# One pipeline over the blocks of the experts, branch hints on four engines, and attention heads in pairs

## The chip, the cores and the metric

The kernel runs on one core of one Trainium2 chip. The metric is the device time in microseconds (us) of one execution. The engines are named as in the profile: PE (TensorE, matmuls and transposes; PEld is its weight load), DVE (VectorE), ACT (ScalarE), POOL (GpSimd), SP (SyncE, which here does little but issue the loads of weights). A name with a q behind it (PEq, DVEq) is that engine's sequencer: branches, register operations and semaphores. All data is float32, for which one matmul shows as two rows of PE; a transpose shows as one.

## The reference, cut to what matters

Two transformer blocks are computed one after the other on 256 tokens of width 1024. The first ends in a mixture of 16 experts, the second has two layers that end in mixtures of 32 experts, over 512 tokens (256 latent, 256 of context) and over 256 tokens. Each token goes to two experts, which the router's scores decide, so how many tokens an expert gets is known only at run time.

```python
def run(args):                       # one block of an expert's tokens
    xb, e = args
    return (jax.nn.silu(xb @ w_gate[e]) * (xb @ w_up[e])) @ w_down[e]
ys = lax.map(run, (xs, block_e)).reshape(cap, d)
return jnp.zeros((n + 1, d), x.dtype).at[slot_tok].add(ys * slot_w[:, None])[:n]
```

w_gate and w_up are 1024x512, w_down is 512x1024: 6 MiB of weights for an expert. The second layer's mixer is an attention with 16 heads of 64: eight query heads that share two heads of keys and values (GQA), and eight "neighbourhood" heads with keys of their own and a bias for each offset in a window. Every head has 256 queries and 512 keys (256 of context, 256 latent):

```python
s = jnp.einsum('bkgqd,bksd->bkgqs', q, k, preferred_element_type=jnp.float32) * ATTN_SCALE
p = jax.nn.softmax(s, axis=-1).astype(v.dtype)
return jnp.einsum('bkgqs,bksd->bkgqd', p, v)
```

## The kernel before, in words

**Stages.** The profiled execution goes through: the first block's mixer and memory attention (0 to about 430 us), its 16 experts (MoE1, to about 745), the conv mixers of the second block (to about 945), 32 experts on 512 tokens (MoE2, to about 1537), projections, the attention (about 1686 to 1774) and its output, then 32 experts on 256 tokens (MoE3, to 2248) and the last combination. In this trace 22 of MoE3's 32 experts have tokens.

**Weights.** SP loads weights in pieces of 1 MiB into a ring of buffers (ring, ringb, and in the MoEs also nrm, x1c and hcT), in a planned order (plan_moe, L1092): for each expert two halves of gate, two of up, two of down. A piece is loaded as soon as its buffer has been given back (ring.free) by an expert that is done with it. For MoE3 (skip=True) the used experts come first in the order, and a load is left out where the count is zero.

**An expert** works on its tokens in blocks of 32. block_up (L1142) multiplies a block's columns with gate and up, 32 matmuls into four column groups of one PSUM bank, and copies the result to a tile u on DVE. block_mid (L1154) turns u on PE (L1158), applies Silu on ACT (L1160), and multiplies on DVE (L1161) into hd. block_down (L1165) is 16 matmuls (L1169) and a copy to a tile y (L1173 on ACT or L1175 on DVE); block 0 is written by a plain DMA that ACT issues (L1177), later blocks by an indirect DMA on POOL (L1179), to places that depend on the counts. There are 105 blocks in this execution: 8 of MoE1's 16 experts have two, 13 of MoE2's 32 have two or three. Token rows come by indirect DMAs (gather, L1205) for four experts at a time and are turned on PE by columns (L1220); a block beyond the second (and the second of MoE3's expert 3) picks its rows by a matmul with a selection matrix instead (columns_32, L1329).

**Branches.** more (L1344) holds the blocks beyond the first in nested Ifs, up to four deep; every engine with instructions in it takes the branch (L1346). The down of block b is passed into the If of block b+1 and stands there behind that block's up; where there is no further block it stands in the Else, or, for the first block of an expert, behind a second branch (L1413, n < 33). ahead (L1340) gives PE alone a hint which way a coming branch will go. In MoE1, MoE2 and for the first three experts of MoE3 the up of the next expert's first block comes ahead of that branch at L1413, so a single-block expert's down runs behind the next expert's up. In the rest of MoE3 every expert stands in an If of its own (L1392, in groups of four under L1432), with its up, its mid and its down in a row, and unused positions are branched over one by one, with their columns (L1220) still done.

**Attention.** 20 steps; step i does the scores of head i (two 64-row matmuls of 512 keys, L2126, and for neighbourhood heads two matmuls that add the bias, L2128), the softmax pieces on DVE and ACT (L2130, L2131), the eight transposes of head i-1 (L2141, copied by ACT L2144 and DVE L2146), the eight value matmuls of head i-2 (L2156, scaled by DVE L2158) and, for every second head, two transposes into oT (L2165).

Of the kernel before, what the change touches and what calls it, by code (L numbers as in the profile page):

```python
# [11 lines left out]
I32 = mybir.dt.int32  # L12
# [78 lines left out]
LAG = (1, 2, 3)  # L91
# [43 lines left out]
def body(tc, a, dbg=lambda n, ap: None, stop=99):  # L135
# [3 lines left out]
    with es:  # L139
# [952 lines left out]
        def plan_moe(m, E, wa, wb, wc, key, after=None, skip=False):  # L1092
# [30 lines left out]
        def moe(m, wa, wb, wc, key, hook=lambda: None, after=lambda e: None, gmul=None, skip=False):  # L1123
# [6 lines left out]
            EQ = E // 4  # L1130
            yb, ya = yslots[0:2 * NT, :], yslots[D:D + 32 * E, :]
# [10 lines left out]
            def block_up(XT, w, tag="u"):  # L1142
# [7 lines left out]
                u = q.tile([128, 256], F32, tag=tag, name="u", bufs=1)  # L1150
# [3 lines left out]
            def block_mid(u, b):  # L1154
# [4 lines left out]
                hd = q.tile([128, 2, 64], F32, tag=f"hd{b}", name="hd", bufs=1)  # L1159
                S.activation(hd, pv[:, :, 0:64], AF.Silu)  # L1160
                V.tensor_tensor(hd, hd, pv[:, :, 64:128], ALU.mult)  # L1161
                return hd[:, 0], hd[:, 1]

            def block_down(hd, w, e, b):
                p = ps("c")  # L1165
                for k in (0, 2, 1, 3):
                    for g in range(4):
                        c = (k % 2) * 1024 + 256 * g
                        T.matmul(p[32 * g:32 * g + 32, 0:256], hd[k % 2][:, 32 * (k // 2):32 * (k // 2) + 32], w[k // 2][:, c:c + 256],  # L1169
# [6 lines left out]
                if b == 0:  # L1176
                    S.dma_start(ya[32 * e:32 * e + 32, :].rearrange("s (g c) -> g s c", g=4), y)  # L1177
                else:
                    G.indirect_dma_start(out=yb.rearrange("r (g c) -> (r g) c", g=4), out_offset=bass.IndirectOffsetOnAxis(ap=iy[:, b - 1, e:e + 1], axis=0),  # L1179
                                         in_=y, in_offset=None, bounds_check=8 * NT - 1, oob_is_err=False)  # L1180
# [33 lines left out]
            def columns(n, XT, sl=slice(0, 128)):  # L1214
                rowsg.remove(n)
                r = gathered[n % 2]
                pa = [ps("c"), ps("c")]
# [27 lines left out]
            u0 = block_up(XTs[0][:, :, 0:32], up_w)  # L1245
# [6 lines left out]
            iy = q.tile([128, NB, E], I32, name="iy")  # L1252

            def blocks():
# [35 lines left out]
                for b in range(NB):  # L1290
                    V.tensor_scalar(iy[:, b, :], obp, 128.0, scol[:, b:b + 1], op0=ALU.mult, op1=ALU.add)
                V.reduce_max(cnt[:, E:], cnt[:, :E], axis=AX.X)
# [7 lines left out]
            def places():  # L1300
                tm = q.tile([128, 256], F32, tag="u", name="tm", bufs=1)[:, :nt * 2 * E].rearrange("p (t k e) -> p t k e", t=nt, k=2)
# [38 lines left out]
            def ahead(e, b, n):  # L1340

                tc.mark_branch_hint_location(f"{key}_{e}_{b}", hint=n > 32 * b, engines=[ET.PE])

            def more(e, b, n, w, w2_, before, other=True):  # L1344

                with tc.If(n > 32 * b, label=f"{key}_{e}_{b}") as cmp:  # L1346
                    if b < NB:
                        ahead(e, b + 1, n)
                    if b == 1 and not (skip and e == 3):
                        u = block_up(XT1[:, :, 32 * (e % 4):32 * (e % 4) + 32], w, "ux")  # L1350
                        before()
                    else:
                        u = block_up(columns_32(e, b, before), w, "ux")
# [15 lines left out]
            def expert(e, up_w, u0, n=None):  # L1369

                i, j = e // 4, e % 4
                by_use = skip and e >= 3
                old = len(due) if by_use else 9
                n1 = None
                if not by_use:
                    dn_w = get(2)
                    hd = block_mid(u0, 0)
                if e == 0:
                    n, n1 = used(0), used(1)
                    ahead(0, 1, n)  # L1380
                    up_1 = get(4)
                    u0 = block_up(XTs[0][:, :, 32:64], up_1)
# [3 lines left out]
                sure = n is not None  # L1386
                n = n if sure else used(e)
                if not by_use:
                    more(e, 1, n, up_w, dn_w, lambda: block_down(hd, dn_w, e, 0), False)
                else:  # L1390
                    up_w, dn_w = get(4), get(2)
                    with ExitStack() if sure else tc.If(n > 0):  # L1392
                        ahead(e, 1, n)
                        hds = block_mid(block_up(XTs[i % 2][:, :, 32 * j:32 * j + 32], up_w), 0)
                        more(e, 1, n, up_w, dn_w, lambda: block_down(hds, dn_w, e, 0))
# [4 lines left out]
                if e == 0:  # L1400
                    up_w = up_1
                    ahead(1, 1, n1)
                elif e + 1 < (3 if skip else E):
                    up_w = get(4)
                    n1 = used(e + 1)
                    ahead(e + 1, 1, n1)
                    u0 = block_up(XTs[((e + 1) // 4) % 2][:, :, 32 * ((e + 1) % 4):32 * ((e + 1) % 4) + 32], up_w)
# [4 lines left out]
                if not by_use:  # L1412
# [862 lines left out]
```

## Time and profile before

| what | value |
| --- | --- |
| median of 3 runs | 2274.81 us (2269.14 to 2281.2) |
| profiled execution | 2280.37 us, span 2278.6 us |
| mean granted clock of PE | 0.88 of full speed |
| busy, share of the span | PE 78%, weight load 49%, DVE 27%, ACT 12%, POOL 11% |
| moved by DMA | 636.5 MB, mean 279 GB/s |

Shares over the whole span say little here, because the stages have different limits: the MoEs stream weights, the stages between them compute on what is there. So the views are read stage by stage.

### The profile page before, as it was taken

The page shows a single profiled execution, that of the slowest core. Times are in us where ns is not written, and L with a number is a line of the kernel's source. Part 1 is how long each engine was busy: PE and PEld are TensorE (multiplying, and loading weights), DVE is VectorE, ACT ScalarE, POOL GpSimd, SP SyncE. Part 2 cuts the span into 40 slices and gives each one's busy share as a digit, 9 for nine tenths or more (in the row PEclk, how much of TensorE's full clock was granted, in tenths as well). Part 3 has the DMA queues.
Part 4 walks back from the last instruction along what each step waited for, and adds up shares of the span by engine and source line. Part 5 has one row for each costly group of instructions (what it writes and reads, how often), then busy time and mean ns, then how long its engine had stood idle before and what let it go on. Part 6 is the DMA issues. An engine that isn't in the chain of part 4 may idle for free. (4 is left out here: it accounts for less than half of the span.)

```text
span 2278.6 us, 39879 instructions
## 1 busy us (share of the span) xinstructions
PE 1777.6 (78%) x15108; PEld 1119.0 (49%) x15108; DVE 624.2 (27%) x1772; ACT 284.4 (12%) x653; POOL 252.6 (11%) x250
## 2 busy tenths in 40 slices
PE   6998999989787699877555787775999867766663
PEld 4856466756555365634223444442856543433432
DVE  5234223334312373421010111005324422110112
ACT  4223111100010101010000000001123110000000
POOL 3010021100000400200000011203010102000001
PEclk9999999999998799788777898997999888887776
DMA  9564664599999698289999787976230564999972
GB/s 342 190 210 160 222 221 163 216 366 352 402 365 352 250 361 316 85 350 373 420 395 391 301 346 319 395 309 238 92 102 10 203 248 177 417 378 380 381 294 81
DMA packets 181086, 636.51 MB, mean 279 GB/s; under 512 B 33122, under 2 KB 70370, under 8 KB 138462
## 3 DMA queue, kind: packets, MB, share of 16 engines
q1 hardware_dynamic: 143660, 573.66, 64.4%
q0 software_dynamic: 14208, 37.56, 4.6%
q10 hardware_dynamic: 22840, 20.36, 2.7%
q8 instruction: 224, 3.67, 0.6%
q14 instruction: 154, 1.26, 0.2%
HBM read 650.18 MB, written 23.36 MB: 296 GB/s over the span
## 5 line engine op out<-in xcount | busy, mean ns | idle before, releaser
L1149 PE MATMUL ps_b<-ring,hT 128*32 128x256 f32 x2256 | 250.5, 461 | 97.8 <-DMA ring<-in_expert_w_up_dram 35.4
L1149 PE MATMUL ps_b<-ringb,hT 128*32 128x256 f32 x1824 | 204.1, 444 | 38.2 <-DMA ringb<-in_expert_w_up_dram 8.6
L1149 PEld LDWEIGHTS ps_b<-ring,hT 128*32 128x32 f32 x2256 | 124.1, 131 | 167.6 <-issue 62.6
L1151 DVE COPY u<-ps_b 128x256 f32<-128x256 f32 x105 | 44.6, 425 | 583.3 <-PE ps_b L1149 582.9
L1169 PE MATMUL ps_c<-ring,hd 128*32 128x256 f32 x1616 | 139.7, 433 | 51.3 <-issue 21.9
L1169 PE MATMUL ps_c<-ringb,hd 128*32 128x256 f32 x1472 | 122.4, 418 | 59.4 <-issue 37.7
L1149 PEld LDWEIGHTS ps_b<-ringb,hT 128*32 128x32 f32 x1824 | 100.3, 128 | 94.2 <-issue 40.3
L1169 PEld LDWEIGHTS ps_c<-ring,hd 128*32 128x32 f32 x1616 | 62.8, 122 | 96.2 <-issue 72.0
L1205 POOL DMA_INDIRECT rowsg<-hrow_d,ix x38 | 38.7, 1019 | 600.8 <-DVE ix L1203 486.9
L1169 PEld LDWEIGHTS ps_c<-ringb,hd 128*32 128x32 f32 x1472 | 55.6, 118 | 95.9 <-issue 73.5
L1179 POOL DMA_INDIRECT yslots<-y,iy x35 | 35.5, 1014 | 554.9 <-ACT y L1173 412.6
L1599 DVE SCALAR_TENSOR_TENSOR ring<-cya,pp,ring 128x256 f32<-128x256 f32 x240 | 96.5, 477 | 0.0
L1173 ACT COPY y<-ps_c 128x256 f32<-128x256 f32 x75 | 27.9, 373 | 473.6 <-PE ps_c L1169 367.2
L1160 ACT ACTIVATE hd<-ps_c 128x128 f32<-128x128 f32 x105 | 29.1, 277 | 430.9 <-PE ps_c L1158 359.3
L412 PE MATMUL ps_a<-hT,ring 128*128 128x256 f32 x320 | 77.1, 401 | 4.3 <-ACT hcT L1720 3.7
L1220 PE MATMUL ps_c<-ident,rowsg 128*128 128x128 f32 x288 | 49.9, 325 | 39.2 <-ACTq L1346 25.8
L1161 DVE TENSOR_TENSOR hd<-hd,ps_c 128x128 f32<-128x128 f32 x105 | 30.1, 287 | 165.0 <-ACT hd L1160 143.6
L1149 PE MATMUL ps_b<-ring,XT 128*32 128x256 f32 x784 | 72.4, 403 | 0.0
L1149 PE MATMUL ps_b<-ringb,XT 128*32 128x256 f32 x800 | 71.8, 401 | 0.7 <-issue 0.7
L412 PEld LDWEIGHTS ps_a<-hT,ring 128*128 128x128 f32 x320 | 63.6, 202 | 14.6 <-ACT hcT L1720 4.1
L1158 PE MATMUL ps_c<-ident,u 128*128 128x128 f32 x210 | 45.2, 298 | 32.8 <-DVE u L1151 24.9
L1220 PEld LDWEIGHTS ps_c<-ident,rowsg 128*128 128x128 f32 x288 | 40.8, 201 | 57.3 <-ACTq L1346 31.8
(746 smaller groups left out, 2802.1 us busy)
## 6 DMA issues: line engine op xcount, KB each, us to landing
ring<-in_expert_w_gate_dram SPq DMA_DIRECT2D x57, 1024.0 KB
ring<-in_expert_w_up_dram SPq DMA_DIRECT2D x57, 1024.0 KB
ring<-in_expert_w_down_dram SPq DMA_DIRECT2D x53, 1024.0 KB
ring<-in_w_dram SPq DMA_DIRECT2D x50, 1024.0 KB
ringb<-in_expert_w_down_dram SPq DMA_DIRECT2D x49, 1024.0 KB
ringb<-in_expert_w_up_dram SPq DMA_DIRECT2D x47, 1024.0 KB
ringb<-in_w_dram SPq DMA_DIRECT2D x46, 1024.0 KB
ringb<-in_expert_w_gate_dram SPq DMA_DIRECT2D x46, 1024.0 KB
```

The lines of the kernel that those rows point to most:

```text
L412: T.matmul(pv[:, c, :], s[k // 4][:, (k % 4) * n + cc * 128:(k % 4) * n + cc * 128 + 128], xT[:, k, :ntok], start=k == 0, stop=k == 7)
L1149: T.matmul(p[32 * g:32 * g + 32, 0:256], XT[:, k, :], ws[:, c:c + 256], start=k == 0, stop=k == 7)
L1151: V.tensor_copy(u, p[:, 0:256])
L1158: T.transpose(pv[:, c, :], u[:, c * 128:(c + 1) * 128], ident)
L1160: S.activation(hd, pv[:, :, 0:64], AF.Silu)
L1161: V.tensor_tensor(hd, hd, pv[:, :, 64:128], ALU.mult)
L1169: T.matmul(p[32 * g:32 * g + 32, 0:256], hd[k % 2][:, 32 * (k // 2):32 * (k // 2) + 32], w[k // 2][:, c:c + 256], start=k == 0, stop=k == 3)
L1173: S.copy(y, p[:, 0:256])
L1179: G.indirect_dma_start(out=yb.rearrange("r (g c) -> (r g) c", g=4), out_offset=bass.IndirectOffsetOnAxis(ap=iy[:, b - 1, e:e + 1], axis=0) ...
L1205: G.indirect_dma_start(out=r, out_offset=None, in_=m.hd_d[:NT, :], in_offset=bass.IndirectOffsetOnAxis(ap=ix, axis=0), bounds_check=NT - 1 ...
L1220: T.transpose(pa[h][:, k * 128:(k + 1) * 128], r[:, bass.ds(4 * h + k, 128, 8)], ident)
L1599: V.scalar_tensor_tensor(acc[:, c, :], ya[:, c, k:k + 256], dww[:, c, k:k + 1], acc[:, c, :], op0=ALU.mult, op1=ALU.add)
```

## The change

One. Loads go in the order gate, up, gate, up, down, down (by halves), and block_up takes its weights in that order. Two. The down of an expert's last block leaves the Ifs and stands, for every expert of all three MoEs, behind the up of the next expert's first block (lead); the Else and the branch at L1413 are gone, hd is one tile. Which block the last one is depends on the counts, so its result is written by POOL's indirect DMA to a place il that about ten new small DVE operations work out once for each MoE. Three. Hints are given to PE, DVE, ACT and POOL. Four. In MoE3 the experts from the fourth on stand in one chain of nested Ifs (tower): the first unused one jumps over all the rest; the up ahead of that jump is done for an expert with no tokens. Five. columns takes the PSUM banks of tag "a" in MoE2 and MoE3. Six. The attention has 16 steps of a pair of heads and half of the queries: two score matmuls whose 64 rows lie in different halves of PE's rows, two matmuls that spread the reciprocal sums (L2151 of the new kernel), and value matmuls with 64 columns for each head of the pair, which give the output already turned, so the transposes of L2165 go.

```diff
             for e in range(E):
-                for w, how, k in ((wa, "(p k)", 4), (wb, "(p k)", 4), (wc, "(k p)", 2)):
-                    for h in range(2):
+                for ws, how, k in (((wa, wb), "(p k)", 4), ((wc,), "(k p)", 2)):
+                    for h, w in ((h, w) for h in range(2) for w in ws):
...
-                        ws = w[2 * (g // 2) + k // 4]
+                        ws = w[2 * (k // 4) + g // 2]
...
                 if b == 0:
                     S.dma_start(ya[32 * e:32 * e + 32, :].rearrange("s (g c) -> g s c", g=4), y)
-                else:
...
+                    return
+                rows_, at = (yslots, il[:, e:e + 1]) if b is None else (yb, iy[:, b - 1, e:e + 1])
+                G.indirect_dma_start(out=rows_.rearrange("r (g c) -> (r g) c", g=4), out_offset=bass.IndirectOffsetOnAxis(ap=at, axis=0),
...
+            def ahead(label, hint):
+                tc.mark_branch_hint_location(f"{key}_{label}", hint=hint, engines=ENG)
+            def more(e, b, n, w, dn):
+                with tc.If(n > 32 * b, label=f"{key}_{e}_{b}"):
                     if b < NB:
-                        ahead(e, b + 1, n)
+                        ahead(f"{e}_{b + 1}", n > 32 * b + 32)
+                    def before():
+                        block_down(dn, e, b - 1)
                     if b == 1 and not (skip and e == 3):
-                        u = block_up(XT1[:, :, 32 * (e % 4):32 * (e % 4) + 32], w, "ux")
+                        u = block_up(XT1[:, :, 32 * (e % 4):32 * (e % 4) + 32], w)
                         before()
...
-                    hds = block_mid(u, b)
-                    def last():
-                        block_down(hds, w2_, e, b)
+                    block_mid(u)
                     if b < NB:
-                        more(e, b + 1, n, w, w2_, last)
-                    else:
-                        last()
-                if other:
-                    with cmp.Else():
-                        before()
+                        more(e, b + 1, n, w, dn)
...
+            def lead(e, n):
+                w = get(4)
+                ahead(f"{e}_1", n > 32)
+                return w, block_up(XTs[(e // 4) % 2][:, :, 32 * (e % 4):32 * (e % 4) + 32], w, u0), n
...
+                more(e, 1, n, up_w, dn_w)
                 ring.hold = e >= E - 1
                 ring.free(*up_w)
...
+                elif e + 1 < E:
+                    nxt = lead(e + 1, used(e + 1))
...
-                if not by_use:
-                    with tc.If(n < 33):
-                        block_down(hd, dn_w, e, 0)
+                block_down(dn_w, e)
...
+            def tower(e, w):
+                with tc.If(w[2] > 0, label=f"{key}_{e}_0"):
+                    w = expert(e, *w)
+                    if e + 1 < E:
+                        tower(e + 1, w)
```

In the attention:

```diff
+        steps = [(c, t) for c in range(8) for t in range(2)]
...
+            p = [ps("a"), ps("b")]
+            for u in range(2):
+                half = slice(64 * u, 64 * u + 64)
+                q_, k_ = (qcT[half, c, tok], kcT[half, c // 2, :]) if c < 4 else (qdT[half, c - 4, tok], kdT[half, c - 4, :])
+                T.matmul(p[u], q_, k_, start=True, stop=c < 4)
...
+            for u in range(2):
+                T.matmul(rp[64 * u:64 * u + 64, 0:128], sm[:, u:u + 1].to_broadcast([128, 64]), ident, start=True, stop=True)
...
+            for kt in range(4):
+                for u in range(2):
...
+                    T.matmul(p[64 * u:64 * u + 64, 0:128], v_, PTs[i % 2][u][:, kt * 128:(kt + 1) * 128], start=kt == 0, stop=kt == 3)
+            V.tensor_tensor(oT[:, c, t * 128:(t + 1) * 128], p[:, 0:128], ri, ALU.mult)
```

Three places of the programs follow (names are those of the buffers in each; an If's body is listed whether it is taken or not). PE before, in MoE1, at the end of an expert: the last matmuls of the next expert's up, the branch at L1413 and the down behind it (L426 belongs to work for a later stage that is put between), then the next expert's turns (L1158) and its branch.

```order
L1149 MATMUL ps_b<-ring_69,hT 32x256 x2
L1149 MATMUL ps_b<-ring_68,hT 32x256 x2
L1413 COMPARE_AND_BRANCH
L1169 MATMUL ps_c<-ringb_1542,hd 32x256 x4
L1169 MATMUL ps_c<-ring_70,hd 32x256 x4
L1169 MATMUL ps_c<-ringb_1542,hd 32x256 x4
L1169 MATMUL ps_c<-ring_70,hd 32x256 x4
L1413 UNCONDITIONAL_BRANCH x2
L426 MATMUL ps_a<-hcT,ringb_1540 128x256 x8
L1158 MATMUL ps_c<-ident,u 128x128 x2
```

PE of the change at the same place.

```order
L1150 MATMUL ps_b<-ring_71,hT 32x256 x2
L1150 MATMUL ps_b<-ring_68,hT 32x256 x2
L1172 MATMUL ps_c<-ringb_1542,hd 32x256 x4
L1172 MATMUL ps_c<-ring_70,hd 32x256 x4
L1172 MATMUL ps_c<-ringb_1542,hd 32x256 x4
L1172 MATMUL ps_c<-ring_70,hd 32x256 x4
L426 MATMUL ps_a<-hcT,ringb_1540 128x256 x8
L1162 MATMUL ps_c<-ident,u_2118 128x128 x2
```

The downs of a last block, of which four stood inside the nested Ifs (one for each count of blocks) and one behind L1413, are a single down behind the next up, with no branch between.

SP before, in MoE2 (ISA rows are semaphore waits): the loads of the second half of one expert and the first half of the next.

```order
L1413 COMPARE_AND_BRANCH
L1413 UNCONDITIONAL_BRANCH x2
L1100 TENSOR_LOAD cnt
L1100 ISA x2
L1108 ISA
L1108 DMA ring_68<-in_expert_w_gate_dram 128x2048
L1108 ISA
L1108 DMA ringb_1544<-in_expert_w_gate_dram 128x2048
L1346 COMPARE_AND_BRANCH x4
L1346 UNCONDITIONAL_BRANCH x5
L1108 ISA
L1108 DMA ring_69<-in_expert_w_up_dram 128x2048
```

SP of the change at the same place.

```order
L1108 DMA ringb_1541<-in_expert_w_down_dram 128x2x1024
L1100 TENSOR_LOAD cnt
L1100 ISA x2
L1108 ISA
L1108 DMA ring_68<-in_expert_w_gate_dram 128x2048
L1108 ISA
L1108 DMA ringb_1544<-in_expert_w_up_dram 128x2048
L1365 COMPARE_AND_BRANCH x4
L1365 UNCONDITIONAL_BRANCH x5
L1108 ISA
L1108 DMA ring_69<-in_expert_w_gate_dram 128x2048
```

The branch of L1413 is gone from SP's row, and gate and up alternate; the loads still stand in the same places against the Ifs.

PE before in the attention, two neighbourhood heads.

```order
L2126 MATMUL ps_a<-ring_70,ring_65 128x512
L2128 MATMUL ps_a<-x1c,keep 128x256
L2126 MATMUL ps_a<-ring_70,ring_65 128x512
L2128 MATMUL ps_a<-x1c,keep 128x256
L2141 MATMUL ps_c<-ident,ring_72 128x128 x8
L2156 MATMUL ps_d<-nrm,ring_71 128x64 x8
L2165 MATMUL ps_c<-ident,oS_30035 128x128 x2
L2126 MATMUL ps_b<-ring_70,ring_65 128x512
L2128 MATMUL ps_b<-x1c,keep 128x256
L2126 MATMUL ps_b<-ring_70,ring_65 128x512
L2128 MATMUL ps_b<-x1c,keep 128x256
```

PE of the change, one step (a pair of neighbourhood heads, half of the queries).

```order
L2124 MATMUL ps_a<-ring_70,ring_65 128x512
L2124 MATMUL ps_b<-ring_70,ring_65 128x512
L2127 MATMUL ps_a<-x1c,keep 128x256
L2127 MATMUL ps_b<-x1c,keep 128x256
L2139 MATMUL ps_c<-ident,ring_72 128x128 x8
L2151 MATMUL ps_c<-ident,asm 64x128 x2
L2157 MATMUL ps_d<-ring_71,nrm 64x128 x8
```

The score matmuls of two heads now stand side by side, the value matmuls write 64 rows of 128 columns instead of 128 rows of 64, the two spreading matmuls are new, and L2165 is gone.

## Rows read from the trace of the kernel before

**Rows 1.** Windows (start:end, length, busy by engine, granted clock, DMA share, GB/s): five stages.

```profile
440.00:740.00 300.00, 250.01 (x2703) 171.71 (x2701) 104.55 (x297) 28.57 (x69) 13.17 (x13) 0.94 0.93 363
975.00:1515.00 540.00, 376.71 (x4994) 209.03 (x4993) 64.38 (x214) 45.19 (x127) 51.54 (x42) 0.84 0.93 372
1845.00:2205.00 360.00, 233.70 (x2819) 136.15 (x2821) 54.69 (x155) 18.27 (x49) 29.85 (x25) 0.81 0.89 358
2205.00:2252.00 47.00, 21.44 (x215) 14.84 (x208) 5.70 (x19) 1.73 (x4) 4.29 (x6) 0.68 0.08 22
1686.00:1774.00 88.00, 87.37 (x498) 59.88 (x499) 39.01 (x80) 37.39 (x90) 10.02 (x8) 1.00 0.17 41
```

**Rows 2.** Windows of 20 us in MoE2, same columns.

```profile
1100.00:1120.00 20.00, 8.35 (x102) 3.91 (x106) 0.71 (x2) 0.65 (x2) 0.00 (x0) 0.67 1.02 420
...
1360.00:1380.00 20.00, 17.41 (x218) 8.94 (x222) 2.29 (x9) 1.63 (x5) 4.47 (x3) 0.83 0.61 249
```

**Rows 3.** Waits of PE in MoE1 (440 to 740): total us, times, longest.

```profile
PE ps_c L1169 <- DVEq L1346: 8.0, 5, 2.0
PE ps_b L1149 <- DVEq L1346: 7.3, 4, 3.2
```

**Rows 4.** Timeline of PE in MoE2: an expert's last down, and what follows.

```profile
1287.00 1.93 PE L1169 MATMUL ps_c<-ring,hd 128*32 128x256 f32 x32 [0.78 <-DVEq L1346]
...
1290.32 0.41 PE L1149 MATMUL ps_b<-ringb,hT 128*32 128x256 f32 x2 [1.39 <-issue]
...
1296.20 0.41 PE L1158 MATMUL ps_c<-ident,u 128*128 128x128 f32 x2 [2.22 <-PEq L1413]
```

**Rows 5.** Waits of PE in MoE2 (975 to 1515).

```profile
PE ps_c L1169 <- issue: 15.7, 4, 4.6
```

**Rows 6.** Waits of SP's queue in MoE2 (975 to 1515).

```profile
SPq L1108 <- PE ps_c L1169: 140.2, 19, 21.8
```

**Rows 7.** Waits of PE in MoE3 (1835 to 2247).

```profile
PE ps_c L1169 <- issue: 41.0, 9, 7.2
PE ps_c L1220 <- ACTq L1346: 17.8, 7, 7.7
PE ps_c L1158 <- DVE u L1151: 14.9, 21, 2.5
```

**Rows 8.** Timeline of SP: the last load of weights that is used.

```profile
2198.98 0.46 SPq L1108 DMA_DIRECT2D ring<-in_expert_w_down_dram  x1
```

**Rows 9.** Timeline of the end of MoE3: last experts, last write, first gather.

```profile
2217.21 2.61 PE L1149 MATMUL ps_b<-ringb,hT 128*32 128x256 f32 x32 [0.63 <-PE ps_c L1169]
...
2225.83 1.02 ACTq L1177 DMA_DIRECT2D yslots<-y  x1
...
2250.50 1.09 POOL L1823 DMA_INDIRECT yb<-yslots,rows  x1 [2.35 <-DVE dg L1837]
```

**Rows 10.** The line L1179, POOL's indirect writes: from issue to landing.

```profile
DMA to landing us min/median/max: 2.5/6.7/7.4
```

**Rows 11.** Timeline of PE in the attention, GQA heads.

```profile
1704.70 1.98 PE L2126 MATMUL ps_b<-nrm,ring 64*128 64x512 f32 x4
1706.62 1.09 PE L2141 MATMUL ps_c<-ident,ring 128*128 128x128 f32 x8
1707.54 1.90 PE L2156 MATMUL ps_d<-nrm,ring 128*128 128x64 f32 x16
1709.37 1.98 PE L2126 MATMUL ps_a<-nrm,ring 64*128 64x512 f32 x4
```

**Rows 12.** Timeline of PE, between the scores of a neighbourhood head.

```profile
1719.98 0.70 PE L2128 MATMUL ps_a<-x1c,keep 128*128 128x256 f32 x2
...
1720.61 1.12 PE L2126 MATMUL ps_a<-ring,ring 64*128 64x512 f32 x2
```

**Rows 13.** The line L1203, a small DVE operation: ns min/median/max.

```profile
L1203 DVE TENSOR_SCALAR ix<-ps_b x38: 149/158/159, 429.2 to 2237.7; 128x1 int32<-128x1 f32 x38
```

**Rows 14.** The line L1346: PE's branches, ns min/median/max.

```profile
L1346 PEldq COMPARE_BRANCH  x142: 67/342/6261, 438.9 to 2223.8; - x142
```

More of the change, by code (lines that the diff above doesn't have):

```diff
@@ L1338, in columns_32 @@
                 return XT.rearrange("p g c r -> p (g c) r")
[L1340 to L1346, printed above, removed]
+            def ahead(label, hint):
+                tc.mark_branch_hint_location(f"{key}_{label}", hint=hint, engines=ENG)
+            def more(e, b, n, w, dn):
+                with tc.If(n > 32 * b, label=f"{key}_{e}_{b}"):
@@ L1378, in expert @@
+            def expert(e, up_w, u, n=None):
+                i, j = e // 4, e % 4
+                block_mid(u)
+                dn_w = get(2)
+                nxt = None
                 if e == 0:
                     n, n1 = used(0), used(1)
-                    ahead(0, 1, n)
-                    up_1 = get(4)
-                    u0 = block_up(XTs[0][:, :, 32:64], up_1)
+                    nxt = lead(1, n1)
+                    ahead("0_1", n > 32)
                     next(blocks_, None)
@@ L1385, in expert @@
                 hook()
[L1386 to L1395, printed above, removed]
+                more(e, 1, n, up_w, dn_w)
                 ring.hold = e >= E - 1
@@ L1411, in expert @@
                     columns(2 * i + 1 + skip, XTs[(i + 1) % 2])
-                if not by_use:
-                    with tc.If(n < 33):
-                        block_down(hd, dn_w, e, 0)
+                if skip and 2 <= e < E - 1:
+                    ahead(f"{e + 1}_0", nxt[2] > 0)
+                block_down(dn_w, e)
                 ring.hold = e >= E - 1
                 ring.free(*dn_w)
-                finish(old)
+                finish()
                 if e == 1:
@@ L1423, in expert @@
                 hook()
-                after(e)
-                return up_w, u0, n1
-            w = up_w, u0
-            for i in range(EQ):
-                if skip and i:
-                    n = used(4 * i)
-                    with tc.If(n > 0):
-                        m.regs.clear()
-                        for e in range(4 * i, 4 * i + 4):
-                            expert(e, None, None, n if e % 4 == 0 else None)
-                        finish()
-                    m.regs.clear()
-                else:
-                    for e in range(4 * i, 4 * i + 4):
-                        w = expert(e, *w)
-                    if skip:
-                        finish()
-            finish()
+                if not (skip and e > 2):
+                    after(e)
+                return nxt
+            def tower(e, w):
[3 more added lines that the diff above has]
+                        tower(e + 1, w)
+            w = up_w, u0
+            for e in range(3 if skip else E):
+                w = expert(e, *w)
+            if skip:
+                after(3)
+                tower(3, w)
             gm = nc.values_load(cnt[0:1, E:E + 1], engines=ENG + [ET.SP], min_val=0, max_val=512)
@@ L2080, in body @@
             p = ps("c")
-            for t in range(2):
-                T.transpose(p[:, t * 128:(t + 1) * 128], kks[r][:, 128 * t:128 * t + 128], ident)
-            S.copy(kcT[:, 256 * r:256 * r + 256], p[:, 0:256])
+            for i in range(4):
+                T.transpose(p[:, i * 128:(i + 1) * 128], kks[r][:, i, :], ident)
+            S.copy(kcT[:, :, 256 * r:256 * r + 256], p.rearrange("p (v t) -> p v t", v=2))
         s = [ring.get(), ring.get()]
@@ L2145, in turned @@
                 else:
-                    V.tensor_copy(dst, p.rearrange("p (k t) -> p k t", k=4))
+                    V.tensor_copy(PTs[i % 2][u], p)
         def values(i):
-            kind, h = heads[i]
+            c, t = steps[i]
             _, sm = state.pop(i)
-            PT = PTs[i % 2]
-            p = PVt[:, 128 * (i % 4):128 * (i % 4) + 128].rearrange("p (t d) -> p t d", t=2)
-            for t in range(2):
-                for kt in range(4):
-                    v_ = vc[:, kt, 64 * (h // 4):64 * (h // 4) + 64] if kind == 0 else vd[:, kt, 64 * h:64 * h + 64]
-                    T.matmul(p[:, t, :], PT[:, kt, t * 128:(t + 1) * 128], v_, start=kt == 0, stop=kt == 3)
@@ L2168, in body @@
         bms = [bias_tiles(h) for h in range(6)]
-        for i in range(16 + 4):
+        for i in range(16 + LAG[1]):
             if i < 16:
@@ L2175, in body @@
                 values(i - LAG[1])
[L2176 to L2180 removed]
+            if i in (10, 11):
+                bms.append(bias_tiles(i - 4))
         def mid():
```

123 lines of the change are left out of this document (53 added, 70 removed).

## The prediction, made before the change was run

> **What bounds the kernel now.** I read the windows by stage first, then the waits of PE and of SP in each MoE, and the timeline last. The reader is to see three kinds of stage.
>
> In the MoEs the loads of weights are the limit where all goes well: in the window from 1100 the DMA engines are at a share of 1.02 and 420 GB/s, PE is busy for 8.35 of 20 us [rows 2]. Later in the same stage it turns round: in the window from 1360 the share is 0.61 and PE busy for 17.41 [rows 2]. Those are the experts with two and three blocks: PE is late, buffers come free late (SP's loads wait 140.2 us in MoE2 for the downs of L1169 [rows 6]), and DMA time is lost for good. Against 1.02 the shares 0.93, 0.93 and 0.89 [rows 1] leave 300 x 0.09 / 1.02 = 26 us unused in MoE1, 48 in MoE2 and 46 in MoE3. That is the most that a smoother PE can win inside the stages.
>
> At the end of MoE3 nothing is loaded any more (share 0.08 [rows 1]): the last useful load is issued at 2198.98 [rows 8], yet the last expert's up starts at 2217.21, its result is sent at 2225.83, and the combination's first gather starts only at 2250.50 [rows 9], because ten unused positions are stepped over.
>
> The attention is bound by PE alone: busy for 87.37 of 88 us at full clock, with DMA at 0.17 [rows 1].
>
> **The change, part by part.**
>
> *Downs out of the branches, MoE2.* After an expert's last mid PE waits 0.78 us for Silu, product and DVE's branch, then does the down, waits 1.39 more at the next up, and 2.22 at L1413 before the next mid [rows 4]. Behind the next up (the down itself is 1.93, an up about twice that) the first of these is covered; the other two belong to branches that go. That is 2.2 us sure (0.78 + 1.39), 4.4 at most, for each of 13 experts with more than one block: 28 to 57 us of PE. The up's buffers are also given back a down earlier. But the gain counts only where DMA stood, 48 us, and the third blocks with their selection matrix stay as long as they are. The waits at downs for "issue" (15.7 [rows 5]) are part of this. I take 25, with 12 and 40 as ends.
>
> *MoE1.* The same for 8 of 16 experts. The rows give 8.0 us before downs and 7.3 before ups, both released by DVE's branch [rows 3]; the first goes with the order, the second partly with the hint: 12, ends 0 and 24. PE is busy for 250 of 300 us there [rows 1], so PE's own work remains the limit.
>
> *MoE3 inside.* 19 experts stand alone in Ifs, with no other work beside their latencies: 41.0 us before downs (9 times, the jump to the Else), 17.8 at columns after a branch, 14.9 waiting for u [rows 7], together 73.7. The tower covers the first and the last with the next up; the hint on ACT bears on the second. Only 46 us can come back, and the waits around selection matrices stay: 27, ends 12 and 42.
>
> *End of MoE3.* From the last result to the first gather there are 2250.50 - 2225.83 = 24.7 us [rows 9]. Now there is one jump and a chain of joins, but the result goes by POOL's indirect DMA, which takes 6.7 us to land [rows 10], and the gather waits for it; with some 2 us for issue and joins, 10 in place of 24.7: 15 less. Before that, the last two experts lag the loads: from the last load (about 5 us to arrive, as two MiB at 420 GB/s take) at 2204 to 2225.8. In a pipeline there are one up, one useless up and one down behind it, at 3.5 + 3.5 + 2 and some waits: 2215, so 10 less. Together 25, ends 12 and 30; the useless up is in it.
>
> *Attention.* A head takes 4.67 us: scores 1.92 (four rows), eight transposes 0.92, values 1.83 [rows 11]. A pair for half of the queries has as many scores and transposes. If the two row halves run at once, scores take 0.99; the value matmuls, on two column halves, 0.9; the spreading matmuls about 0.2 and two switches between 64 and 128 rows 0.2 each: 0.99 + 0.92 + 0.9 + 0.2 + 0.4 = 3.4, with some slack 3.6. No row shows two halves of 64 rows at once. For columns the rows do show it: the down's 32 rows of 128x256 take 1.93 [rows 4], while two such rows alone take 0.63 to the next start, the switch included [rows 12]; one by one they would be several times as long. So I take overlap. 16 steps at 3.6, and 0.85 for the two bias matmuls in eight of them, are 64 to 68 us with the ends, against 88: 19 less, ends 26 less and, without any overlap (1.92 + 0.92 + 1.83 + 0.9 a step), 9 more. DVE and ACT have some 2.6 us of work for a step, which is less than PE's.
>
> The Trainium skill, "TensorEngine Tiling (Array Packing)", section Key Properties, says that a change of tiling mode drains TensorE. The 0.63 us for two bias rows agree with a small price for each switch, and no row here shows a larger one.
>
> *What is added.* Ten small DVE operations for il, at 0.15 each [rows 13], double for wider ones, lie at the start of each MoE, partly under the second expert's up: 0 to 3 us, I take 1.5 for each, and 1.5 for hints and registers on three engines: 6 in all. The writes by POOL cost about 1 us of POOL each and 6.7 to land; with two tiles y and blocks 5 us or more apart they are covered, and the cost is the end of each MoE, counted above for MoE3. The order gate, up, gate, up lets an up start one load (2.5 us) sooner, but its second half waits for the fourth load in both orders, so: nothing. The other banks for columns take no work away and add none: nothing either, and a wait for a bank would show at L1220.
>
> **The sum.** 12 + 25 + 27 + 25 + 19 - 6 = 102 us less. The profiled execution is 2280.4, so 2178 by it; it lies 5.6 above the median, so against the runs shown 2173.
>
> **The rivals.**
>
> *Branches keep their price.* In this case the change hardly does what it says. PE had its hints already, and its branches at L1346 still take 0.342 us in the median and up to 6.26 [rows 14]; so a hint need not be worth anything on other engines, and a downs' place behind the next up may just move the jump's wait ahead of that up. Then MoE1 gives 0, MoE2 8, MoE3 10, its end 15, attention 19, less 6: 46 less, 2229. For it: the 1.39 before an up is put down to "issue" [rows 4]. Against it: the number of branches really falls. The skill's "Runtime: NRT & Kernel Launch", section Instruction fetch mechanics, speaks for this one: a taken branch whose target is not near has to fetch instructions first, and that holds for the tower's long jump as well. The 41.0 us in nine waits agree that such a jump is dear.
>
> *All of it comes back.* MoEs run at the rate of the window from 1100: 26 + 48 + 46 less, 30 at the end, 26 in the attention, nothing added: 176 at most, some 150 likely: 2125. Against it: the stretches with three-block experts, where PE itself is busy for 17.41 of 20.
>
> *The heads do not run in pairs.* Attention 9 more instead of 19 less, the rest as forecast: 2201. The place to see it is the time of two scores, 1.9 instead of 1.0.
>
> *Slower.* Every last block's result now stands in POOL's queue, between the gathers of the next experts' rows and their columns. If a gather is held until a down is done, then lands 7 us later, and PE waits for it at columns, that costs up to 8 us for each group of four experts, 20 groups: 160. With the other parts as forecast it needs more than 102, or 5 us a group, to make the kernel slower; say 2300. Against it: a gather is asked for two groups ahead.
>
> **How the numbers follow.** Forecast 0.52, branches keep their price 0.19, all of it 0.10, no pairs 0.10, slower 0.05, about no change (several small ones together) 0.04. The time is the forecast's, 2173. For 8 in 10 the range reaches up to the case of the branches, to 2240, and down to 2125. About 0.5% (11 us) is what a measurement of this kernel can tell from no change. Faster than that: 0.91; within it: 0.04; slower: 0.05.
>
> **What the profile of the changed kernel would show.** Right: no wait before a down for issue or a branch; the window that holds MoE3 at a DMA share near 0.95; a last gather some 10 us after the last down; two scores of a pair in about 1 us and an attention of 64 to 70 us. Wrong: the same idle time of PE now before the ups, or at columns with POOL's gather as releaser; DMA shares as before, at 0.93 and 0.89; a last gather still 20 us behind. The sum would be wrong above all if DMA, at 1.02 already, has other small traffic that keeps it below that rate, or if three-block experts alone decide how late the loads are.

## The result, and the profile after

The changed kernel takes 2219.37 us in the median of 4 runs (2206.81 to 2221.01), the kernel before 2271.97 (4 runs): a ratio of 0.975 (95% interval 0.970 to 0.980). That is faster by 53 us, where 102 were forecast; the time lies in the stated range, in its upper half. The profiled execution has a span of 2216.2 us against 2278.6.

The profiled execution of the kernel before lies 8 us above the median of its runs, that of the changed kernel 1 us below, so some 10 of the 62 us between the two spans are the spread of the runs.

Where the 62 us came from is read by stages. A MoE stage is taken from the first row of its ups to the last of its downs; the other stages lie between. (So measured, MoE1 ends at 757.2 in the kernel before and MoE2 starts at 960.1, not at about 745 and 945.)

```
stage (us)          before   after   forecast   measured
start to MoE1        424.1   419.5        0        -4.6
MoE1                 333.1   330.8      -12        -2.3
to MoE2              202.9   205.2        0        +2.3
MoE2                 576.7   575.1      -25        -1.6
to MoE3 (attention)  290.5   265.4      -19       -25.1
MoE3                 398.0   383.5      -37       -14.5
its end              53.3    36.7      -15       -16.6
```

(The 6 us put down for what is added are not in it; the 37 are the 27 inside MoE3 and the 10 of its last experts.) The attention and the end came as forecast. The three MoEs gave 18 of 74; the 2 us in MoE1 and in MoE2 are no more than such a stage differs between traces of nearly the same kernel (328.0 and 330.8 in MoE1 with hints on PE alone and on four engines). Their windows, in the columns of [rows 1], and one of 88 us that ends with the attention, which runs from 1679.2 to 1743.8:

```profile
437.00:735.00 298.00, 248.24 (x2704) 169.65 (x2702) 103.84 (x294) 29.24 (x71) 22.04 (x21) 0.93 0.94 366
970.00:1510.00 540.00, 391.33 (x5106) 218.36 (x5098) 67.38 (x217) 44.60 (x130) 70.05 (x60) 0.85 0.94 376
1812.00:2160.00 348.00, 232.05 (x2878) 131.24 (x2876) 57.12 (x167) 19.22 (x51) 46.16 (x41) 0.79 0.92 371
1655.00:1743.00 88.00, 85.67 (x591) 52.65 (x591) 36.22 (x79) 37.23 (x101) 10.04 (x8) 0.98 0.20 55
```

The DMA shares rose from 0.93, 0.93 and 0.89 to 0.94, 0.94 and 0.92 only: the loads are held up nearly as much as before. By what, the waits of PE in MoE2 tell (970 to 1510; L1150 is the up's line now, L1172 the down's, L1365 the branch over the extra blocks), and then those in MoE3 (1812 to 2160):

```profile
PE ps_b L1150 <- DVEq L1365: 32.3, 8, 6.5
PE ps_b L1150 <- issue: 22.8, 12, 4.2
PE ps_b L1150 <- PEq L1365: 14.2, 3, 5.9
...
PE ps_b L1150 <- SPq L1365: 11.1, 6, 2.3
```

```profile
PE ps_b L1150 <- PEq L1365: 40.6, 8, 5.8
PE ps_a L1224 <- PEq L1365: 24.2, 5, 5.3
```

No down stands in these two lists with "issue" any more, as in [rows 5, 7] before. Nor does a wait at columns (L1224) for a gather of POOL, the sign of the rival "slower": there too it is PE's own branch. But the ups wait, and for the same branch. Over the whole run it shows in what ended the idle time ahead of the downs (first) and of the ups, of PE and its weight load together: before,

```profile
  issue: 211.7, 195
...
  issue: 135.4, 365
...
  PEq L1346: 46.7, 15
...
  DVEq L1346: 20.4, 8
```

and after:

```profile
  issue: 21.9, 61
...
  issue: 263.1, 568
  PEq L1365: 159.5, 36
  DVEq L1365: 58.4, 20
```

So 190 us ahead of the downs went, and ahead of the ups 151 came back under the two branches and 128 more under "issue". For PE alone, added up from the traces: its waits ahead of the downs fell from 114 us to 11, those ahead of the ups rose from 142 to 236. The part of them that falls into branches of PE of over 1 us went from 63 to 2 ahead of the downs, from 33 to 109 ahead of the ups, and from 14 to 31 ahead of columns. PE's own branches in MoE3, in min, median and max of their length in ns, before and after:

```profile
L1346 PEldq COMPARE_BRANCH  x45: 67/371/6067, 1843.0 to 2223.8; - x45
```

```profile
L1365 PEldq COMPARE_BRANCH  x34: 65/4054/6958, 1816.1 to 2155.0; - x34
```

The reader is to see the median: 0.37 us has become 4.05. Added up from the trace, PE's branches of over 1 us take 17.5, 93.3 and 82.1 us in the three MoEs and just behind them before, and 14.6, 93.0 and 115.6 after, in the last 22 of them. On DVE, ACT, POOL and SP no branch of either kernel takes over 0.3 us.

The attention, two steps of GQA heads, against [rows 11]: two scores of a pair in 1.06 us (1689.41 to 1690.47, ps_a and ps_b at once), a step in 3.32. From the first score to the last value matmul the attention takes 64.6 us, 87.7 before.

```profile
1689.41 0.69 PE L2124 MATMUL ps_a<-kcT,ring 64*128 64x512 f32 x1
1689.41 0.69 PE L2124 MATMUL ps_b<-kcT,ring 64*128 64x512 f32 x1
...
1690.47 1.09 PE L2139 MATMUL ps_c<-ident,nrm 128*128 128x128 f32 x8
1691.49 0.44 PE L2151 MATMUL ps_c<-ident,asm 128*64 128x128 f32 x4
1691.76 1.04 PE L2157 MATMUL ps_d<-ring,nrm 128*64 128x128 f32 x16
1692.73 0.69 PE L2124 MATMUL ps_a<-kcT,ring 64*128 64x512 f32 x1
```

The end of MoE3, against [rows 9]: the last result is sent at 2180.29, the first gather follows 8.9 us later, not 24.7.

```profile
2180.29 0.98 POOL L1183 DMA_INDIRECT yslots<-y,il  x1 [9.24 <-DVE y L1178]
...
2189.19 1.03 POOL L1822 DMA_INDIRECT yb<-yslots,rows  x1 [3.09 <-DVE dg L1836]
```

### The profile page after: what moved, and what is told of

Its sections match the earlier page's. It is cut to its first block, busy times and chain, and to the rows that moved or that the text cites. A ratio compares the mean times of both kernels' runs of the same rounds, so it can differ in the third digit from the quotient of the medians.

```text
span 2216.2 us, 39872 instructions
## 1 busy us (share of the span) xinstructions
PE 1756.0 (79%) x15200; PEld 1094.9 (49%) x15200; DVE 626.1 (28%) x1792; ACT 279.9 (13%) x659; POOL 296.8 (13%) x292
## 5 line engine op out<-in xcount | busy, mean ns | idle before, releaser
L1150 PE MATMUL ps_b<-ring,hT 128*32 128x256 f32 x2304 | 279.8, 492 | 119.9 <-DVEq L1365 36.1
L1150 PE MATMUL ps_b<-ringb,hT 128*32 128x256 f32 x1824 | 230.5, 485 | 99.6 <-PEq L1365 33.6
L1150 PEld LDWEIGHTS ps_b<-ring,hT 128*32 128x32 f32 x2304 | 132.2, 138 | 209.1 <-issue 133.3
L1183 POOL DMA_INDIRECT yslots<-y,il x70 | 71.0, 1015 | 1003.4 <-ACT y L1176 393.5
L1150 PEld LDWEIGHTS ps_b<-ringb,hT 128*32 128x32 f32 x1824 | 108.5, 137 | 170.2 <-issue 78.9
L1153 DVE COPY u<-ps_b 128x256 f32<-128x256 f32 x71 | 30.1, 425 | 508.7 <-PE ps_b L1150 508.7
L1172 PE MATMUL ps_c<-ring,hd 128*32 128x256 f32 x1616 | 127.7, 397 | 7.6 <-DVEq L1365 3.2
L1172 PE MATMUL ps_c<-ringb,hd 128*32 128x256 f32 x1472 | 114.4, 388 | 3.4 <-issue 1.4
L1172 PEld LDWEIGHTS ps_c<-ring,hd 128*32 128x32 f32 x1616 | 60.2, 114 | 45.9 <-issue 12.1
L412 PE MATMUL ps_a<-hT,ring 128*128 128x256 f32 x320 | 76.0, 397 | 3.6 <-ACT hcT L1719 3.5
L1150 PE MATMUL ps_b<-ring,XT 128*32 128x256 f32 x784 | 74.4, 389 | 0.0
L1172 PEld LDWEIGHTS ps_c<-ringb,hd 128*32 128x32 f32 x1472 | 56.6, 113 | 35.7 <-issue 8.0
L1150 PE MATMUL ps_b<-ringb,XT 128*32 128x256 f32 x800 | 71.4, 383 | 0.0
L412 PEld LDWEIGHTS ps_a<-hT,ring 128*128 128x128 f32 x320 | 62.9, 201 | 13.5 <-ACT hcT L1719 3.9
L1224 PE MATMUL ps_a<-ident,rowsg 128*128 128x128 f32 x216 | 36.5, 321 | 33.5 <-PEq L1365 33.2
L426 PE MATMUL ps_a<-hT,ring 128*128 128x256 f32 x256 | 61.0, 393 | 0.0
L426 PEld LDWEIGHTS ps_a<-hT,ring 128*128 128x128 f32 x256 | 48.6, 195 | 18.1 <-issue 10.1
L1224 PEld LDWEIGHTS ps_a<-ident,rowsg 128*128 128x128 f32 x216 | 30.3, 201 | 42.3 <-issue 37.4
```

The lines of the kernel that those rows point to most:

```text
L412: T.matmul(pv[:, c, :], s[k // 4][:, (k % 4) * n + cc * 128:(k % 4) * n + cc * 128 + 128], xT[:, k, :ntok], start=k == 0, stop=k == 7)
L426: T.matmul(pv[:, c, :], s[:, k * 256 + c * 128:k * 256 + c * 128 + 128], xT[:, k, :], start=k == 0, stop=k == 7)
L1153: V.tensor_copy(u, p[:, 0:256])
L1172: T.matmul(p[32 * g:32 * g + 32, 0:256], hd[:, k % 2, 32 * (k // 2):32 * (k // 2) + 32], w[k // 2][:, c:c + 256], start=k == 0, stop=k == 3)
L1183: G.indirect_dma_start(out=rows_.rearrange("r (g c) -> (r g) c", g=4), out_offset=bass.IndirectOffsetOnAxis(ap=at, axis=0), in_=y, in_offs ...
L1224: T.transpose(pa[h][:, k * 128:(k + 1) * 128], r[:, bass.ds(4 * h + k, 128, 8)], ident)
```

## The experiments

The theory that the profile after suggests (A): PE has to jump over the code of the extra blocks for most experts, the instructions behind the jump come late, and PE has nothing queued that could run meanwhile. The change left these jumps as they were and took away the downs that stood behind them. The rival (B): at the end of the Ifs PE waits until DVE has passed its own branch, which stands in DVE's queue behind Silu and product; so their latency is paid ahead of the up in place of ahead of the down. All ratios are to the kernel before, run on the same chip.

**Hints.** On PE alone, and none:

```diff
-                tc.mark_branch_hint_location(f"{key}_{label}", hint=hint, engines=ENG)
+                tc.mark_branch_hint_location(f"{key}_{label}", hint=hint, engines=[ET.PE])
```

(For none, the line is left out.)

> The changed kernel with hints on PE alone. Theory A (what is left of the gain goes into PE's own jumps, which wait for their instructions): DVE, ACT and POOL spend under 0.1 us in each of their branches, so their hints are worth nothing: within 6 us of the changed kernel's 2219. Theory B (PE waits at the end of the Ifs until DVE, which is behind Silu and product, has passed its branch): also within 10 us. Rival C (the hints on the other engines are what the change lives on in the experts): 20 us or more above it, about 2240.

Measured: 2211.61, ratio 0.9737 (0.971 to 0.976), the same as the changed kernel. The hints on DVE, ACT and POOL are worth nothing.

> The changed kernel with no hint on any engine. Theory A: the hinted jumps of MoE1 and MoE2 that now take under 0.5 us (about ten of 32 in MoE2) become like the others, 4 to 6 us; PE's branches rise from 223 us in all to 300 or more, the time by 10 to 30 us, to 2230 to 2250; MoE3's experts, whose jump over the extra blocks has no hint in the changed kernel either, stay as they are. If hints do nothing at all: 2219 within 8, and the branches as long as before.

Measured: 2312.13, ratio 1.018 (1.017 to 1.020), 93 us above the changed kernel. PE's branches of over 1 us rise to 75.1, 183.8 and 130.3 us; MoE1 takes 34 us more, MoE2 49, MoE3 7. So PE's hints are worth far more than I gave them, and time goes with the jumps, about half of what they grow by: where the changed kernel has hints, leaving them out costs, and in MoE3 hardly. There, from the fourth expert on, the trace of the changed kernel holds no hint for the first jump over the extra blocks: the chain puts another branch between the hint's place and the jump, and the instruction is not issued.

**The length of what is jumped over.**

```diff
-        NB = 4
+        NB = 2
```

> The changed kernel with code for at most two extra blocks of an expert in place of four (it leaves out experts with more than 96 tokens, which these inputs do not have). The code that a one-block expert jumps over is half as long. Theory A: PE's branches fall from 223 us in all to under 120, and the time by 15 to 40 us, to 2180 to 2205. Theory B: DVE's and SP's branches are passed at the same moments, so the time stays within 8 us of 2219.

Measured: 2187.56, ratio 0.9628 (0.961 to 0.965). MoE3 is shorter by 20.6 us, MoE2 by 8.6, MoE1 by 4.7. But the sums of the branches went to 21.8, 70.8 and 95.3: 188 us in all from 223, where I expected under 120, and more in MoE1 than the 14.6 of the changed kernel. Most jumps of a one-block expert in MoE3 still take about 6 us; what became cheaper there is above all the second jump, out of the Ifs after an extra block: four of these take 4 to 5.3 us in the changed kernel (5.3 at 1922.1), 0.4 to 2.3 here. So the time says A, and the 35 us that the branches lost are near the 32 that the time lost; but that half the code makes each jump half as long, as I expected, is not so.

> The kernel before with code for two extra blocks instead of four (leaves out the same experts). Its branches on PE take 193 us in all, against 223 after the change. If the long jumps cost the kernel before as much as the changed one: 2235 to 2250, about 30 less. If in the kernel before the downs that stand at the jumps' targets and the other waits cover them: 2260 to 2275, and the jump is a cost that the change brought onto the path.

Measured: 2270.84 with 10 runs, ratio 0.998 (0.995 to 1.001). The same edit gives nothing in the kernel before, where the branches of over 1 us fall from 193 us to 177 in all. That is the second case: the jump is a cost that the change brought onto the path. Which waits covered it before, no run shows.

**The wait for DVE.**

```diff
-                p = ps("b")
+                p = ps("b" if u is None or E == 16 else "d")
```

> The changed kernel in which the up of an expert's first block, in MoE2 and MoE3, writes a PSUM bank of its own (tag d) in place of one of the two banks (tag b) that the blocks inside the Ifs use too, so PE need not wait at the end of the Ifs until DVE has passed its branch. Theory B (the latency of Silu, product and DVE's branch is not hidden but paid ahead of the up): PE's waits before L1150 released by DVE's branch (32.3 us in MoE2, 8.7 in MoE3) go, and the time falls by 10 to 30 us, to 2190 to 2209. Theory A (PE's own jump, which takes longer, is what counts): the waits change their name to PE's branch or to issue, and the time stays within 8 us of 2215.

Measured: 2199.48, ratio 0.9667 (0.963 to 0.971); the kernel with the later hint (below), timed beside it, is at 2217.79. MoE2 is 8.7 us shorter, MoE3 12.4. The wait of 32.3 us for DVE's branch before an up is gone in MoE2:

```profile
PE ps_d L1150 <- issue: 29.8, 14, 4.9
PE ps_d L1150 <- PEq L1365: 20.1, 8, 5.3
...
PE ps_d L1150 <- DMA ringb<-in_expert_w_up_dram: 14.2, 7, 4.9
```

So B holds too, for a part: of the 32.3 us some passed to the jump (14.2 became 20.1, issue 22.8 became 29.8), some to late loads and columns, and the stage won 8.7. In MoE3 more was won (12.4) than the 8.7 us that PE waited there for DVE's branch; its waits for the jump fell as well (40.6 became 32.1), and why they did is not shown.

**When the hint is given.** In MoE1 and MoE2 ahead of the down (some 5 us later); and in MoE3 one If for four experts, so that three of four have a hint:

```diff
-                ahead(f"{e}_1", n > 32)
+                if skip or e < 2:
+                    ahead(f"{e}_1", n > 32)
...
+                if not skip and 0 < e < E - 1:
+                    ahead(f"{e + 1}_1", nxt[2] > 32)
                 block_down(dn_w, e)
```

> The changed kernel in which, in MoE1 and MoE2, the hint for the next expert's jump is given ahead of the down instead of ahead of the next expert's up, so about 5 us later and with 64 instead of some 190 instructions of PE between hint and jump. If a hint is lost because PE's own code goes on too far before the jump: the stalls fall (93 us in MoE2 to under 60) and the time by 5 to 20 us. If the stalls come because the instructions take long to arrive: they get longer (to 110 to 150 us), and the time rises by 10 to 25 us.

Measured: 2217.79, ratio 0.9716 (0.968 to 0.975). The stalls got longer, 122.8 us in MoE2 in place of 93.0, as the second case says, but the time did not move, where that case had 10 to 25 us more. So some of PE's stalls cost nothing; that loads which are late anyway cover them is likely and not shown.

```diff
...
                 with tc.If(w[2] > 0, label=f"{key}_{e}_0"):
-                    w = expert(e, *w)
-                    if e + 1 < E:
-                        tower(e + 1, w)
+                    for x in range(e, e + 4):
+                        w = expert(x, *w)
+                    if e + 4 < E:
+                        tower(e + 4, w)
...
```

> The changed kernel with MoE3's chain of Ifs in steps of four experts in place of one; up to three unused experts are computed for nothing, into places that nothing reads. In the changed kernel no hint is issued for the jump over the extra blocks in MoE3 (the program has another branch between), and 22 of its jumps take 5.3 us each. With one If for four experts three of four experts have a hint. Theory A: PE's branches in MoE3 fall from 115.6 us to 40 to 70, MoE3 gets 10 to 25 us shorter inside, its end up to 16 longer for the two unused experts of the last group; in all 0 to 20 less, 2195 to 2215. If hints do not work in MoE3's traffic of loads: 5 to 15 more.

Measured: 2222.75, ratio 0.974 (0.970 to 0.978): no gain. PE's branches in MoE3 fell to 81.5 us (40 to 70 expected): where a hint is issued a jump takes anything from 0.4 us to 6.1. Two experts are computed for nothing. A number from these traces bears on both: from a hint to the end of a jump that still waited, the median is 11.0 us in MoE2 of the changed kernel (21 jumps), 10.7 in MoE3 of this one (10 jumps). A hint some 6 us ahead, which is where an up and a down put it, thus mostly leaves 4 to 5 us to wait, against 6.0 without a hint. Where 10.9 us or more lie between the two, eight of eleven jumps in MoE2 of the changed kernel are free (under 0.5 us); the other three, with hints 11.5 to 14.7 us ahead, still wait 2.0 to 3.9. The 11 us are no fixed length of a fetch: with the later hint the moved hints stand 1.3 to 4.0 us ahead, and the jumps behind them in MoE2 take 2.5 to 6.2 us, with a median of 5.1 against 6.0 without any hint. A hint as late as that saves little.

**The pairs by themselves**, on the kernel before, and the changed kernel with the old attention:

> The kernel before with the paired heads of the change and nothing else. The profile after has 25 us less between MoE2 and MoE3. If this is the attention alone: 2247 within 5 (25 less), with two scores of a pair in about 1 us. If a part of it comes from other things (an earlier end of MoE2's experts' loads): 2255 to 2260.

> The changed kernel with the attention of the kernel before. The stage between MoE2 and MoE3 then is as long as before (290 instead of 265 us), so 2237 to 2243 if nothing else moves. The pairs alone on the kernel before gave 22.6 us in that stage but only 9.7 in all; if the other half is given back in the experts' stages by something that goes with the pairs (another place of the code behind them), it is 2225 to 2232 here.

Measured: 2262.82, ratio 0.9957 (0.994 to 0.998, 8 runs), and 2238.81, ratio 0.982 (0.979 to 0.986). The stage is shorter by 22.6 us and longer by 24.2, as it should be. In all the pairs are worth about 21 on the changed kernel (against the 2217.79 timed beside it), but only 10 on the kernel before. Why half was lost there isn't settled: its MoEs took 2 to 3 us more each, and no wait stands out. The two spans that these stages come from differ by 18.5 us, since the profiled execution of the kernel before lies 8 us above its median; so a part of the difference is the spread of the runs.

**The order of the loads:** gate, gate, up, up again, with the matching weights in block_up.

> The changed kernel with loads and weights in the order of before (gate, gate, up, up). The prediction put this edit at nothing: 2217 within 8. If an up that can start one load earlier is worth something where loads are late: 5 to 15 more than the changed kernel.

Measured: 2209.69, ratio 0.972 (0.968 to 0.977): no difference.

**Together.** Two extra blocks, the bank of its own, hints on PE:

> The changed kernel with three edits at once: code for two extra blocks instead of four (it leaves out experts with more than 96 tokens, which these inputs do not have), the bank of its own for a first block's up in MoE2 and MoE3, hints on PE alone. Alone they gave about 31, 18 and 0 to 8 us. If PE's jump (A) and the wait for DVE at the join (B) are two costs in a row, the gains add up: 2165 to 2175. If they are one and the same wait seen from two sides, the larger one is all there is: 2180 to 2190. Loads at their full rate in MoE2 and MoE3 would allow about 2150.

Measured: 2177.55, ratio 0.958 (0.954 to 0.962), 42 us below the changed kernel and between the two cases: the two waits add up in part. MoE1 is at 323.0 us, MoE2 at 562.6 and MoE3 at 356.0: 10, 14 and 42 us below the kernel before, where 12, 25 and 37 were forecast. In MoE3 (1778.6 to 2134.5 here) the DMA share is 0.95 over 255 us, from 66 us behind its start on, where the kernel before and the changed one have 0.89 and 0.92 at the same distance from its start:

```profile
1845.00:2100.00 255.00, 172.91 (x2288) 97.92 (x2288) 37.23 (x102) 11.54 (x32) 29.15 (x27) 0.82 0.95 390
```

Last, on top of these, MoE3's chain turned round:

```diff
+                    with tc.If(n1 < 1) as cmp:
+                        block_down(dn_w, e)
+                    with cmp.Else():
+                        rest()
+                        expert(e + 1, *nxt)
```

> The kernel of the three edits (two extra blocks, a bank of its own, hints on PE) with MoE3's chain turned round: the test whether the next expert has tokens stands ahead of that expert's up; where it has none, only the down of the last expert is done, else comes the up, with the hint for the jump over its extra blocks, then the down and the rest. So every such jump in MoE3 has a hint about 6 us ahead, and no up is done for nothing; each expert has one more short jump, over the down of the other arm. Theory A: PE's branches in MoE3 fall from 97.5 us to 30 to 65, MoE3 gets 8 to 20 us shorter, in all 2157 to 2170. If the new short jump has to fetch as well: 4 to 6 us for each expert again, the sum stays at 90 or more, and the time at 2175 to 2190.

Measured: 2184.76 (6 runs), ratio 0.955 (0.951 to 0.959): not to be told from the one before it. The branches' sum stays at 92.0 us, as the second case says: the jumps over the extra blocks fell from 91.0 us to 63.7, but the new short jumps over the down take 23.4, five of them 3.5 to 5.1 each. The hint is issued now, and a jump that follows it 6.1 us later still waits 5.6:

```profile
L2264 PEldq BRANCH_PREFETCH_HINT  x1: 40/40/40, 1955.1 to 1955.1; - x1
```

```profile
L1365 PEldq COMPARE_BRANCH  x1: 5563/5563/5563, 1961.2 to 1961.2; - x1
```

That is 11.7 us from hint to end; over the 15 such jumps of the chain the median is 11.0. So the hints took off a part of each jump, and the test that they needed cost about as much.

## Why the prediction was right in sign and too large

*Attention: right.* 19 forecast, 22 to 25 found in the stage, with the pieces as worked out: two scores of a pair 1.06 us (0.99 forecast), a step 3.32 (3.6), the whole 64.6 (64 to 68). No step shows a switch of tiling that costs more than the forecast gave it.

*End of MoE3: right,* 8.9 us from the last result to the gather (10 forecast), 16.6 less for the stage behind it (15). The 10 for its last experts stand in the MoE3 row and can't be read by themselves.

*The order of the loads:* right, nothing to be told from noise. *What is added:* the 6 us were not measured by themselves.

*MoE1, MoE2, MoE3: the step that failed* is "the first of these is covered; the other two belong to branches that go". Neither is true. Of the waits in [rows 4], Silu's and the product's latency is not covered, since the next up stands behind the join, where it waits for DVE's branch (32.3 us in MoE2; a bank of its own takes this away). And the branch that costs is not the one at L1413, as the 2.22 us in [rows 4] made it seem: of branches over 1 us it has two in MoE2, 5.4 us, one of them that of [rows 4], and none inside MoE1 and MoE3. It is the jump over the extra blocks, which stays: before, a wait for it lay ahead of a down (63 us of PE's idle time in the whole run), after the change it lies ahead of the next up (109). So 74 us became 18. The runs bear it out from the other side: with shorter code, the up's bank and hints on PE alone the time is 2177.55, near the 2173 forecast. What I set down as the rival "branches keep their price" (46 less, 2229) is what happened in the MoEs, with the attention and the end as in the forecast; it had 0.19 and should have had more. Its sentence "a hint need not be worth anything on other engines" was right (2211.61 with hints on PE alone); what nothing in the prediction priced is PE's own hints, 93 us in the changed kernel. The Trainium skill ("Runtime: NRT & Kernel Launch", section Instruction fetch mechanics) says that a taken branch to a target that is not near waits until the target has been fetched. The 14 jumps over extra blocks without a hint in MoE3, at a median of 6.0 us, agree; I should have given the rule more weight.

A further term was left out, and no run separates it: PE's clock. Where an up follows a long jump, the granted clock is 0.50 (1.2 GHz) from 1960.7 to 1965.0, behind 5.7 us in which PE was busy for 1.79, and 1.00 (2.4 GHz) in the 2 us after. Over all of MoE3 it is 0.82 before, 0.80 after, and 0.83 with code for two extra blocks.

*What was read wrongly in the rows:* [rows 14] show a median of 0.34 us for PE's branches and a longest of 6.26, and I took the median. The sum of PE's branches above 1 us, 193 us (167 of them at L1346 inside the MoEs), would have told that there was a cost larger than all the DMA time to be won, 120 us.

Whether the loads, which fill the DMA engines, make the instructions behind a jump come late is not shown: no run changed the traffic alone. Behind MoE3 of the kernel before, with the DMA share near 0.1, three branches (2228.9 to 2246.8) still take 3.5 to 5.0 us.

## What to carry to other kernels

A wait at a branch doesn't go away when the work behind the branch is moved; look what stands behind the jump then, and put there something that needs neither the jump nor the other engine's branch. Sum the long tail of a sequencer's branches, not their median. A prefetch hint saves more the further ahead it stands: here little at 1.3 to 4 us, a part at 6, and mostly the whole jump from about 11 us on, with no other branch between.

## What was not expected of the hardware

- From a hint to the end of a jump that still waits: a median of 11.0 us in MoE2 (21 jumps; from 4 to 18), while a jump without a hint in MoE3 takes 6.0 us from its own start. Why a hint does not bring the jump's end to 6 us behind the hint stays open.
- Only PE's branches stall: in MoE3 of the changed kernel its long ones mostly take 4 to 7 us; of DVE, ACT, POOL and SP none takes more than 0.5 us in any run, with or without hints.
- Two 64-row matmuls of 512 columns in different halves of PE's rows run at once: the pair takes 1.06 us, two after another 1.92 [rows 11].
